# Building a gate table from contiguous float32 one-hots, with 62 instead of 48 expert chunks parked ahead

## The chip, the core and the metric

The kernel runs on one core of one Trainium2 chip. The metric is the device time of one execution, in microseconds. The median of three runs before the change is 1922.45 us (1918.22 to 1923.83).

Engine names as in the profile: PE multiplies matrices (PEld is its loading of the stationary operand), DVE and ACT work element by element, POOL issues the indirect gathers here, SP issues all other DMAs.

## The reference

One encoder layer on 512 tokens of width 1024: a mixer of attention and a gated recurrence, then a retrieval layer over 16384 single-neuron experts, then a gated addition of a per-layer embedding. The change is in the retrieval layer. Cut to what matters:

```python
q = (ht @ w_q).reshape(T, PEER_HEADS, 2, PEER_DKEY // 2)
s = jnp.einsum('thpc,hpnc->thpn', q, sub_keys)
v1, i1 = lax.top_k(s[:, :, 0], K); v2, i2 = lax.top_k(s[:, :, 1], K)     # K = 16 of 128 keys
top_s, pos = lax.top_k(v1[..., :, None] + v2[..., None, :], K)           # 16 pairs a head
idx = i1 * 128 + i2 at pos;  g = softmax(top_s)
a = einsum('thkd,td->thk', u[idx], x)        # 8 heads x 16 experts a token
w = gelu(a) * g
out = einsum('thk,thkd->td', w, v[idx])
```

After it, for every token, x + sigmoid(rmsnorm(x) @ ple_gate) * (p @ ple_proj).

## The kernel before

Tokens are worked in four blocks of 128. Matmuls of full precision are made of three matmuls over operands split into a high and a low part (mm3, lines 133 to 136; split, lines 138 to 141: ACT rounds to the high part, DVE subtracts for the low one).

The retrieval layer treats the blocks in two ways. **Block 0** gathers: for each of its 128 (head, rank) slots one indirect DMA brings 128 rows of u (slot_u), DVE multiplies them with the token's normed vector and sums; later a second one brings the rows of v (slot_v, line 898) and DVE accumulates them into acc. **Blocks 1 to 3** (384 tokens) are dense: the 16384 experts are taken as 128 chunks of 128. For each chunk, dense_a (line 776) computes all products with u in PSUM (pa, 24 matmuls with 384 columns) and takes their gelu (ge). w_prep (line 985) multiplies ge by the chunk's gate table (the softmax weight where a token selected the expert, else zero), splits the product and the chunk of v, and w_mm (line 1010) multiplies them into the six accumulators po (18 matmuls with 512 columns a chunk).

The gate table is built by build (line 850) for one block at a time and written to HBM (gdram), because it is needed chunk by chunk but is made token by token. For each token it is an outer product: a one-hot of the first index (gL) and a one-hot of the second index scaled by the softmax weight (gR), contracted over the 128 slots by one float32 matmul into PSUM (pg; two instructions each). For 8 tokens at a time, DVE compares an iota with the indices into gL (float32, token-major) and gO (bf16, the token innermost), ACT scales gO into gR one token at a time, PE multiplies, ACT moves four tokens' results from pg into the block buffer gs, where the token is innermost, and every 32 tokens gs goes out by DMA. gs has one buffer.

While the tables are built, PE also works through chunks of the first product. Their ge can't be used yet, so the first SP = 48 of them are *parked*: written to HBM (adram, line 958) and read back in w_prep (ges, line 1000). The other 80 are *fresh*, made in the main loop shortly before their use; at most PRE of them wait in SBUF. chunk_order spreads the parked ones over the main loop. Program order follows units of estimated cost: topk and build yield cost units, and one more chunk is emitted for every APACE units (line 967); GPACE, GSTART, GS2 and GP2 pace the u gathers in the same way. The order on each engine is then laid out by the framework's planner, with raised priority for the splits of u (HPU) and the gelu (HPG).

The main loop (line 1018) runs over the 128 chunks: w_prep, fresh chunks as due, w_mm, then u and v gathers of block 0 as due. The table is read back 8 chunks at a time into one buffer (GC, B_GC; line 992). At iteration IT1 = 118 all remaining gathers are emitted, the pools of the first product are closed, and the per-layer embedding's part begins, with block 0's norm and its first gate. The last four chunks' matmuls (LASTN) are done at the end, block by block, so that each block's norm runs beside the next one's matmuls; then the remaining gates run.

Of the kernel before, what the change touches and what calls it, by code (L numbers as in the profile page):

```python
# [28 lines left out]
C_ID, C_IOTA, C_COS, C_SIN, C_RST = 0, 128, 256, 384, 512  # L29
# [3 lines left out]
UEND = 8  # L33
WG = 8
LASTN = 4
GC = 8
B_GC = 1
# [11 lines left out]
PRE = 8  # L49
SP = 48  # L50
TQ = 8
APACE = 3.3
# [7 lines left out]
IT1 = 118  # L60
WLAG = 4
# [24 lines left out]
def const_arrays():  # L86
    c = np.zeros((128, C_END), np.float32)
# [6 lines left out]
    for off, fn in ((C_COS, np.cos), (C_SIN, np.sin)):  # L94
        c[:, off:off + 128] = fn(ang).astype(np.float32).reshape(NT, 128, 32).transpose(1, 0, 2).reshape(128, 128)
    rst = np.ones((8, 128), np.float32)
    rst[:, 0] = 0.0
    c[:, C_RST:C_END] = rst.reshape(-1)[None]
# [27 lines left out]
def body(nc, tc, I, out, taps=None, stop=99):  # L126
# [17 lines left out]
    with contextlib.ExitStack() as top:  # L144
        glob = top.enter_context(tc.tile_pool(name="glob", bufs=1))
        cst = glob.tile([128, C_END], F32, name="cst")
# [49 lines left out]
        if True:  # L196
# [4 lines left out]
            hT_l = fp.tile([128, ND, T], F32R, name="hT_l")  # L201
            ysp = [[fp.tile([128, 4, T], F32R, name=f"{nm}{p}") for p in "hl"] for nm in "oy"]
# [11 lines left out]
            with tc.tile_pool(name="n1", side="right", bufs=1) as n1:  # L214
# [4 lines left out]
                DM.dma_start(cst[:, 0:C_COS], I["cst"][:, 0:C_COS])  # L219
# [7 lines left out]
                DM.dma_start(cst[:, C_COS:C_END], I["cst"][:, C_COS:C_END])  # L227
# [105 lines left out]
            def hgrn_head(h):  # L333
# [5 lines left out]
                V.tensor_tensor_scan(SC.rearrange(fl), cst[:, C_RST:C_END], LF.rearrange(fl), 0.0, OP.mult, OP.add)  # L339
# [144 lines left out]
            for tb in range(NT):  # L484
                for (src, dst, H, o, gg) in ((aq[:, tb, :], qr, 8, 0, qn_g), (akv[:, tb, 0:128], kr, 2, 8, kn_g)):
# [7 lines left out]
                    co, si = [cst[:, off + 32 * tb:off + 32 * tb + 32].rearrange("p (a i) -> p a i", a=2)[:, None]  # L493
# [159 lines left out]
        v8s = [pp.tile([128, 16, 16], F32, name=f"v8_{tb}") for tb in range(NT)]  # L653
        i8s = [pp.tile([128, 16, 16], U32, name=f"i8_{tb}") for tb in range(NT)]
        with s5:
# [49 lines left out]
            ul_st = contextlib.ExitStack()  # L705
            up = [ul_st.enter_context(tc.tile_pool(name="ustr0", side="left", **LR))]
# [50 lines left out]
def peer(nc, tc, I, out, xd, cst, gains, norm_T1, rstd_of, split, mm3, tap, stop, pp, ha, la, h2n, v8s, i8s, st, top,  # L757
# [8 lines left out]
    if True:  # L766
# [83 lines left out]
        def build(kp, bp, ps, tb, i_f, g_o, iob):  # L850
# [3 lines left out]
            tij = kp.tile([128, 2, 128], BF16, name="tij", tag="tij")  # L854
# [3 lines left out]
            for b in range(128 // GB):  # L858
                gs = bp.tile([128, 128, GB], F32, name="gs", tag="gs", bufs=1)
                for q8 in range(GB // TQ):  # L860
                    t0 = b * GB + q8 * TQ
                    LL = bp.tile([128, TQ, 128], F32, name="gL", tag="gL")
                    OO = bp.tile([128, 128, TQ], BF16, name="gO", tag="gO")
                    RR = bp.tile([128, TQ, 128], F32, name="gR", tag="gR")
                    V.tensor_tensor(LL, iob[:, :, 0][:, None, :].to_broadcast([128, TQ, 128]),
                                    tij[:, 0, t0:t0 + TQ, None].to_broadcast([128, TQ, 128]), op=OP.is_equal)
                    V.tensor_tensor(OO, iob, tij[:, 1, None, t0:t0 + TQ].to_broadcast([128, 128, TQ]), op=OP.is_equal)  # L867
                    for t in range(TQ):
                        S.activation(RR[:, t, :], OO[:, :, t], AF.Copy, scale=gr[:, t0 + t:t0 + t + 1])  # L869
                    for q4 in range(TQ // 4):  # L870
                        pg = ps.tile([128, 4, 128], F32, name="pg", tag="pg")
                        for w in range(4):
                            t = q4 * 4 + w
                            PE.matmul(pg[:, w, :], RR[:, t, :], LL[:, t, :], start=True, stop=True)  # L874
                        o = q8 * TQ + 4 * q4
                        S.activation(gs[:, :, o:o + 4].rearrange("p i t -> p t i"), pg, AF.Copy)  # L876
                    yield TQ * 0.21 + 0.1
# [4 lines left out]

        def gather(src, k, tag):
            t = gt.tile([128, D], F32, name=tag, tag=tag)
# [35 lines left out]
        with s7:  # L920
# [3 lines left out]
            iob = kp.tile([128, 128, TQ], BF16, name="iob")  # L924
            V.tensor_copy(iob, iota[:, :, None].to_broadcast([128, 128, TQ]))
# [17 lines left out]
            def units():  # L943
                yield from sel(0)
                yield from sel(1)
                for tb in (1, 2, 3):
                    gens = [build(kp, bp, ps, tb, *sels[tb], iob)]
                    if tb < 3:
                        gens.append(sel(tb + 1))
                    yield from zipped(*gens)  # L950
# [28 lines left out]

        vp = ys.enter_context(tc.tile_pool(name="vstr", side="right", bufs=2, reuse_waits="tile"))  # L980
# [3 lines left out]
        N0 = na  # L984
        def w_prep(it):
            c = it
# [11 lines left out]
            if spilled:  # L998
                ge = vp.tile([128, TD], F32, name="ges", tag="ges", bufs=B_GE)
                DM.dma_start(ge, ad[spidx[c]])  # L1000
# [17 lines left out]
        for it in range(128):  # L1018
# [9 lines left out]
            if it < IT1:  # L1028
                if it >= G0:
                    gathers(GW + (it + 1 - G0) * (128 + WLAG - GW) / (IT1 - UEND - G0), VLEAD + (it + 1 - G0) * 128 / (IT1 - G0), ops[0], ops[5])  # L1030
            if it == IT1:
                gathers(999, 999, ops[0], ops[5])
# [29 lines left out]
                V.tensor_tensor(X[0], X[0], acc, op=OP.add)  # L1062
# [27 lines left out]
                norm_T1(pe2[0], ps1, "p1", X[0], 2, h3h, h3l, "n3", 0, B_XN)  # L1090
                gate(0, 0, *wg0, ps1, "p1")
        for tb in range(3):
# [5 lines left out]
            norm_T1(pe2[0], ps1, "p1", X[tb + TB0], 2, h3h, h3l, "n3", tb + TB0, B_XN)  # L1098
        ys.close()
        with contextlib.ExitStack() as e2:  # L1100
            pe2.append(e2.enter_context(tc.tile_pool(name="ple3", side="right", **LR)))
            ps = e2.enter_context(tc.psum_pool(name="psp", side="right", bufs=4, reuse_waits="tile"))
            for n in range(4):
                w = wg0 if n == 0 else load_wg(n)
                for tb in range(1 if n == 0 else 0, NT):
# [59 lines left out]
```

## Time and profile before

| | us |
|---|---|
| median of three runs | 1922.45 |
| the profiled execution | 1921.56 |
| its span | 1919.8 |
| PE busy in the span | 1841.0 |
| PEld busy | 1619.2 |
| DVE busy | 1416.3 |
| ACT busy | 982.5 |
| POOL busy | 374.3 |

The profile is of one execution. A matmul's busy time runs from its start to its modelled end and matmuls overlap, so a busy PE is not a PE at its peak; the distance from one matmul's start to the next's tells more. The granted TensorE clock was 0.994 over the span. The DMA share is the mean busy share of the core's 16 DMA engines. An idle time is put down to what ended it. In each of the profile's rows, L and a number is a line of the kernel.

### The profile page before, as it was taken

To read this page: it belongs to the slowest core of one execution; us is meant where nothing else is said; L and a number is where in the kernel's file an instruction comes from. 1 tells how busy PE (TensorE), PEld (TensorE's weight loads), DVE (VectorE), ACT (ScalarE), POOL (GpSimd) and SP (SyncE) were. 2 spreads that over 40 slices of the span, in tenths; PEclk is the share of its full clock that TensorE was granted. 3 is DMA by queue.
4 is the path that set the end of the run, shared out by engine and by line. 5 is a ranking of instruction groups with operands and counts; after the bars stand their busy time and mean duration, and the time that the engine had idled before them with its cause. 6 is when DMAs were issued, how large, how long until landed. Compare 5 with 4: busy or idle time off the path is not lost.

```text
span 1919.8 us, 27163 instructions
## 1 busy us (share of the span) xinstructions
PE 1841.0 (96%) x9989; PEld 1619.2 (84%) x9989; DVE 1416.3 (74%) x2893; ACT 982.5 (51%) x1561; POOL 374.3 (19%) x260
## 2 busy tenths in 40 slices
PE   6999999999999999888889999999999999999998
PEld 5997888888887988787778888888888888888888
DVE  3689787444898999988746778887777777656464
ACT  5755656432433589999994334333333333333443
POOL 0000000000000322214301334443354443201000
PEclk9999999999999999999999999999999999999999
DMA  4212100433321776777748998988999988765512
GB/s 161 78 55 78 45 12 23 132 108 129 119 84 60 268 252 239 270 262 266 260 168 307 335 338 318 326 327 319 327 332 341 319 306 324 265 220 177 191 58 86
DMA packets 133941, 397.44 MB, mean 207 GB/s; under 512 B 12848, under 2 KB 52016, under 8 KB 132144
## 3 DMA queue, kind: packets, MB, share of 16 engines
q1 hardware_dynamic: 96944, 261.48, 38.7%
q0 software_dynamic: 36864, 134.23, 19.6%
q8 instruction: 78, 1.28, 0.3%
q14 instruction: 55, 0.45, 0.1%
HBM read 356.86 MB, written 38.80 MB: 206 GB/s over the span
## 4 chain that ended last, share of the span: by engine, by line
PE 45%; ACT 9%; DMA 2%; DVE 1%; issue 0%; ACTq 0%; SPq 0%
PE po L136 9%; PE po L135 9%; PE po L134 9%; PE pa L136 5%; PE pa L135 5%; PE pa L134 5%; ACT gR L869 4%; ACT gs L876 3%; DMA gdram<-gs 1%; ACT u_h L139 1%; PE pg L134 1%; PE pg L136 1%; PE pg L135 1%; DMA gchg<-gdram 1%; ACT ge L784 0%
## 5 line engine op out<-in xcount | busy, mean ns | idle before, releaser
L885 POOL DMA_INDIRECT gu<-in_peer_u_dram,idxg x128 | 191.7, 1498 | 1131.8 <-DVE cd L808 659.5
L136 PE MATMUL pa<-ha,u_l 128*128 128x384 f32 x1024 | 349.4, 341 | 5.5 <-DVE u_l L140 5.5
L134 PE MATMUL pa<-ha,u_h 128*128 128x384 f32 x1024 | 349.3, 341 | 2.2 <-ACT u_h L139 1.8
L135 PE MATMUL pa<-la,u_h 128*128 128x384 f32 x1024 | 348.7, 341 | 0.0
L134 PE MATMUL po<-v_h,w_h 128*128 128x512 f32 x768 | 299.5, 390 | 1.9 <-ACT w_h L139 1.9
L135 PE MATMUL po<-v_l,w_h 128*128 128x512 f32 x768 | 300.8, 392 | 0.0
L136 PE MATMUL po<-v_h,w_l 128*128 128x512 f32 x768 | 300.7, 392 | 0.0
L139 ACT ACTIVATE u_h<-u_raw 128x1024 fp32r<-128x1024 f32 x128 | 136.4, 1066 | 205.8 <-PE pa L135 198.2
L885 POOL DMA_INDIRECT gv<-in_peer_v_dram,idxg x128 | 182.4, 1425 | 239.9 <-DVE acc L900 208.2
L140 DVE TENSOR_TENSOR u_l<-u_raw,u_h 128x1024 fp32r<-128x1024 f32 x128 | 156.2, 1221 | 90.7 <-ACT u_h L139 90.6
L136 PEld LDWEIGHTS pa<-ha,u_l 128*128 128x128 f32 x1024 | 193.3, 189 | 7.6 <-DVE u_l L140 7.4
L134 PEld LDWEIGHTS pa<-ha,u_h 128*128 128x128 f32 x1024 | 193.5, 189 | 6.0 <-ACT u_h L139 2.5
L135 PEld LDWEIGHTS pa<-la,u_h 128*128 128x128 f32 x1024 | 193.3, 189 | 2.8
L874 PE MATMUL pg<-gL,gR 128*128 128x128 f32 x768 | 145.7, 305 | 34.8 <-ACT gs L876 18.3
L140 DVE TENSOR_TENSOR v_l<-v_raw,v_h 128x1024 fp32r<-128x1024 f32 x128 | 155.9, 1219 | 25.5 <-ACT v_h L139 25.5
L869 ACT ACTIVATE gR<-gO,gr 128x128 f32<-128x128 bf16 x384 | 170.0, 547 | 4.1 <-DVE gO L867 4.0
L134 PEld LDWEIGHTS po<-v_h,w_h 128*128 128x128 f32 x768 | 144.5, 188 | 30.8 <-ACT w_h L139 2.2
L136 PEld LDWEIGHTS po<-v_h,w_l 128*128 128x128 f32 x768 | 144.6, 188 | 30.3
L874 PEld LDWEIGHTS pg<-gL,gR 128*128 128x128 f32 x768 | 108.4, 191 | 71.9 <-ACT gR L869 33.5
L135 PEld LDWEIGHTS po<-v_l,w_h 128*128 128x128 f32 x768 | 144.5, 188 | 28.7
L900 DVE SCALAR_TENSOR_TENSOR acc<-gv,aa,acc 128x1024 f32<-128x1024 f32 x128 | 163.7, 1279 | 5.3 <-DMA gv<-in_peer_v_dram,idxg 4.9
L891 DVE SCALAR_TENSOR_TENSOR gu<-gu,h2n 128x1024 f32<-128x1024 f32 x128 | 155.5, 1217 | 6.5 <-DMA gu<-in_peer_u_dram,idxg 6.5
(323 smaller groups left out, 3448.7 us busy)
## 6 DMA issues: line engine op xcount, KB each, us to landing
u_raw<-in_u_t_dram SPq DMA_DIRECT2D x128, 512.0 KB, 5.4
v_raw<-in_peer_v_dram SPq DMA_DIRECT2D x128, 512.0 KB, 6.7
gdram<-gs SPq DMA_DIRECT2D x12, 2048.0 KB, 7.8
gchg<-gdram SPq DMA_DIRECT2D x16, 1536.0 KB, 12.6
w_raw<-in_w_in_dram SPq DMA_DIRECT2D x42, 512.0 KB, 3.6
adram<-ge SPq DMA_DIRECT2D x48, 192.0 KB, 3.3
ges<-adram SPq DMA_DIRECT2D x48, 192.0 KB, 6.5
wq_raw<-in_peer_wq_dram SPq DMA_DIRECT2D x16, 512.0 KB, 3.5
```

What stands on the lines that cost most here:

```text
L134: PE.matmul(ps, lh, rh, start=first, stop=False)
L135: PE.matmul(ps, lh, rl, start=False, stop=False)
L136: PE.matmul(ps, ll, rh, start=False, stop=last)
L139: ins = S.activation(hi, raw, AF.Copy)
L140: V.tensor_tensor(lo, raw, hi.bitcast(F32), op=OP.subtract)
L869: S.activation(RR[:, t, :], OO[:, :, t], AF.Copy, scale=gr[:, t0 + t:t0 + t + 1])
L874: PE.matmul(pg[:, w, :], RR[:, t, :], LL[:, t, :], start=True, stop=True)
L876: S.activation(gs[:, :, o:o + 4].rearrange("p i t -> p t i"), pg, AF.Copy)
L885: G.indirect_dma_start(out=t, out_offset=None, in_=src, in_offset=bass.IndirectOffsetOnAxis(ap=idxg[:, k:k + 1], axis=0))
L891: V.scalar_tensor_tensor(t, t, 1.0, h2n, op0=OP.mult, op1=OP.mult, accum_out=aa[:, k:k + 1])
L900: V.scalar_tensor_tensor(acc, t, aa[:, k:k + 1], acc, op0=OP.mult, op1=OP.add)
```

## The change

The constants table is split: the identity and the iota stay for the whole kernel, the rotary tables and the scan's resets go to a tile cfr that lives only as long as the first part. The top-8 lists move into a pool that is released with the first product's buffers. In build, gL and gO become one float32 tile gE, made by one compare from the float32 iota, the token outside and the key innermost for both indices; gR reads it contiguously; the pg tile has the token innermost, so each matmul writes every fourth float of a bank, and the eviction writes runs of four floats. The bf16 copy of the iota is gone.

62 chunks are parked instead of 48, at one per 2.6 cost units instead of 3.3, and PRE is 7. Parked chunks are asked for three iterations ahead of use. The table is read back four chunks at a time into two buffers. The v gathers get a pool of their own that outlives the first product's; they are spread up to iteration 127, those of u up to IT1; block 0's add, norm and first gate come after block 1's last matmuls and norm, and the gate that runs between is block 1's.

```diff
-GC = 8
-B_GC = 1
+GC = 4
+B_GC = 2
...
-PRE = 8
-SP = 48
+PRE = 7
+SP = 62
 TQ = 8
-APACE = 3.3
+APACE = 2.6
...
+VEND = 128
+GLEAD = 3
...
-        cst = glob.tile([128, C_END], F32, name="cst")
+        cst = glob.tile([128, C_FR], F32, name="cst")
...
+            cfr = fp.tile([128, C_END], F32, name="cfr")
...
-        v8s = [pp.tile([128, 16, 16], F32, name=f"v8_{tb}") for tb in range(NT)]
-        i8s = [pp.tile([128, 16, 16], U32, name=f"i8_{tb}") for tb in range(NT)]
...
+            tp = ul_st.enter_context(tc.tile_pool(name="top8", side="left", **LR))
+            v8s = [tp.tile([128, 16, 16], F32, name=f"v8_{tb}") for tb in range(NT)]
+            i8s = [tp.tile([128, 16, 16], U32, name=f"i8_{tb}") for tb in range(NT)]
...
-            tij = kp.tile([128, 2, 128], BF16, name="tij", tag="tij")
+            tij = kp.tile([128, 2, 128], F32, name="tij", tag="tij")
...
-                    LL = bp.tile([128, TQ, 128], F32, name="gL", tag="gL")
-                    OO = bp.tile([128, 128, TQ], BF16, name="gO", tag="gO")
+                    EE = bp.tile([128, 2, TQ, 128], F32, name="gE", tag="gE")
                     RR = bp.tile([128, TQ, 128], F32, name="gR", tag="gR")
-                    V.tensor_tensor(LL, iob[:, :, 0][:, None, :].to_broadcast([128, TQ, 128]),
-                                    tij[:, 0, t0:t0 + TQ, None].to_broadcast([128, TQ, 128]), op=OP.is_equal)
-                    V.tensor_tensor(OO, iob, tij[:, 1, None, t0:t0 + TQ].to_broadcast([128, 128, TQ]), op=OP.is_equal)
+                    V.tensor_tensor(EE, iota[:, None, None, :].to_broadcast([128, 2, TQ, 128]),
+                                    tij[:, :, t0:t0 + TQ, None].to_broadcast([128, 2, TQ, 128]), op=OP.is_equal)
                     for t in range(TQ):
-                        S.activation(RR[:, t, :], OO[:, :, t], AF.Copy, scale=gr[:, t0 + t:t0 + t + 1])
-                    for q4 in range(TQ // 4):
-                        pg = ps.tile([128, 4, 128], F32, name="pg", tag="pg")
+                        S.activation(RR[:, t, :], EE[:, 1, t, :], AF.Copy, scale=gr[:, t0 + t:t0 + t + 1])
+                    for q in range(TQ // 4):
+                        pg = ps.tile([128, 128, 4], F32, name="pg", tag="pg")
                         for w in range(4):
-                            t = q4 * 4 + w
-                            PE.matmul(pg[:, w, :], RR[:, t, :], LL[:, t, :], start=True, stop=True)
-                        o = q8 * TQ + 4 * q4
-                        S.activation(gs[:, :, o:o + 4].rearrange("p i t -> p t i"), pg, AF.Copy)
+                            t = 4 * q + w
+                            PE.matmul(pg[:, :, w], RR[:, t, :], EE[:, 0, t, :], start=True, stop=True)
+                        o = q8 * TQ + 4 * q
+                        S.activation(gs[:, :, o:o + 4], pg, AF.Copy)
...
-            iob = kp.tile([128, 128, TQ], BF16, name="iob")
-            V.tensor_copy(iob, iota[:, :, None].to_broadcast([128, 128, TQ]))
...
+        gpool["gv"] = ys.enter_context(tc.tile_pool(name="gathv", side="right", bufs=B_G, reuse_waits="tile"))
...
         def w_prep(it):
+            nonlocal nb
+            while nb < min(128, it + 1 + GLEAD):
+                if nb in spidx:
+                    back[nb] = vp.tile([128, TD], F32, name="ges", tag="ges", bufs=B_GE)
+                    DM.dma_start(back[nb], ad[spidx[nb]])
+                nb += 1
...
-                ge = vp.tile([128, TD], F32, name="ges", tag="ges", bufs=B_GE)
-                DM.dma_start(ge, ad[spidx[c]])
+                ge = back.pop(c)
...
-            if it < IT1:
-                if it >= G0:
-                    gathers(GW + (it + 1 - G0) * (128 + WLAG - GW) / (IT1 - UEND - G0), VLEAD + (it + 1 - G0) * 128 / (IT1 - G0), ops[0], ops[5])
+            if it >= G0:
+                gathers(999 if it >= IT1 else GW + (it + 1 - G0) * (128 + WLAG - GW) / (IT1 - G0), (it + 1 - G0) * 128 / (VEND - G0), ops[0], ops[5])
             if it == IT1:
-                gathers(999, 999, ops[0], ops[5])
                 ul_st.close()
...
-                V.tensor_tensor(X[0], X[0], acc, op=OP.add)
...
-                norm_T1(pe2[0], ps1, "p1", X[0], 2, h3h, h3l, "n3", 0, B_XN)
-                gate(0, 0, *wg0, ps1, "p1")
...
             norm_T1(pe2[0], ps1, "p1", X[tb + TB0], 2, h3h, h3l, "n3", tb + TB0, B_XN)
+            if tb == 0:
+                gathers(999, 999)
+                V.tensor_tensor(X[0], X[0], acc, op=OP.add)
+                norm_T1(pe2[0], ps1, "p1", X[0], 2, h3h, h3l, "n3", 0, B_XN)
+                gate(TB0, 0, *wg0, ps1, "p1")
...
-                for tb in range(1 if n == 0 else 0, NT):
+                for tb in (0, 2, 3) if n == 0 else range(NT):
                     gate(tb, n, *w, ps, "pg2")
```

More of the change, by code (lines that the diff above doesn't have):

```diff
@@ L27 @@
 NCELL = sum(ROW_N)
-C_ID, C_IOTA, C_COS, C_SIN, C_RST = 0, 128, 256, 384, 512
+C_ID, C_IOTA, C_FR = 0, 128, 256
+C_COS, C_SIN, C_RST = 0, 128, 256
 C_END = C_RST + 2 * T
@@ L86, in const_arrays @@
 def const_arrays():
-    c = np.zeros((128, C_END), np.float32)
+    c = np.zeros((128, C_FR + C_END), np.float32)
     c[:, C_ID:C_ID + 128] = np.eye(128, dtype=np.float32)
@@ L94, in const_arrays @@
     for off, fn in ((C_COS, np.cos), (C_SIN, np.sin)):
-        c[:, off:off + 128] = fn(ang).astype(np.float32).reshape(NT, 128, 32).transpose(1, 0, 2).reshape(128, 128)
+        c[:, C_FR + off:C_FR + off + 128] = fn(ang).astype(np.float32).reshape(NT, 128, 32).transpose(1, 0, 2).reshape(128, 128)
     rst = np.ones((8, 128), np.float32)
     rst[:, 0] = 0.0
-    c[:, C_RST:C_END] = rst.reshape(-1)[None]
+    c[:, C_FR + C_RST:] = rst.reshape(-1)[None]
     s = np.arange(128)
@@ L218, in body @@
                 DM.dma_start(x1[0], I["x"][0:128, :])
-                DM.dma_start(cst[:, 0:C_COS], I["cst"][:, 0:C_COS])
+                DM.dma_start(cst, I["cst"][:, 0:C_FR])
                 DM.dma_start(gains, I["gains"])
@@ L226, in body @@
                 pre[1280] = wtile(w_in[10], (8, 128))
-                DM.dma_start(cst[:, C_COS:C_END], I["cst"][:, C_COS:C_END])
+                DM.dma_start(cfr, I["cst"][:, C_FR:C_FR + C_END])
                 r = rstd_of(n1, ss, NT, 1.0 / D, "n1")
@@ L338, in hgrn_head @@
                 fl = "p a t -> p (a t)"
-                V.tensor_tensor_scan(SC.rearrange(fl), cst[:, C_RST:C_END], LF.rearrange(fl), 0.0, OP.mult, OP.add)
+                V.tensor_tensor_scan(SC.rearrange(fl), cfr[:, C_RST:C_END], LF.rearrange(fl), 0.0, OP.mult, OP.add)
                 S4 = SC.rearrange("p a (c j) -> p a c j", c=4)
@@ L492, in body @@
                     x1, x2 = s5[:, :, :, 0, :], s5[:, :, :, 1, :]
-                    co, si = [cst[:, off + 32 * tb:off + 32 * tb + 32].rearrange("p (a i) -> p a i", a=2)[:, None]
+                    co, si = [cfr[:, off + 32 * tb:off + 32 * tb + 32].rearrange("p (a i) -> p a i", a=2)[:, None]
                               .to_broadcast([128, H, 2, 16]) for off in (C_COS, C_SIN)]
@@ L848, in topk, with build @@
             yield 0.6
-        def build(kp, bp, ps, tb, i_f, g_o, iob):
+        def build(kp, bp, ps, tb, i_f, g_o):
             pt = ps.tile([128, 3, 128], F32, name="pt3", tag="pt3", bufs=1)
@@ L881, in peer @@
         un, vn = I["peer_u"], I["peer_v"]
+        gpool = {"gu": gt}
         def gather(src, k, tag):
-            t = gt.tile([128, D], F32, name=tag, tag=tag)
+            t = gpool[tag].tile([128, D], F32, name=tag, tag=tag)
             G.indirect_dma_start(out=t, out_offset=None, in_=src,
@@ L946, in units @@
                 for tb in (1, 2, 3):
-                    gens = [build(kp, bp, ps, tb, *sels[tb], iob)]
+                    gens = [build(kp, bp, ps, tb, *sels[tb])]
                     if tb < 3:
@@ L984, in peer @@
         N0 = na
+        back = {}
+        nb = 0
         def w_prep(it):
+            nonlocal nb
[4 more added lines that the diff above has]
+                nb += 1
             c = it
```

## The prediction

> **What bounds the kernel now.** I read the busy times by stretch first, because the page's whole-span shares mix stages with different limits. Columns: stretch, its length, then busy us (and instruction count) of PE, PEld, DVE, ACT and POOL, the granted clock, the DMA share, GB/s.
>
> ```profile
> 620.00:685.00 65.00, 62.44 (x348) 60.29 (x348) 63.22 (x247) 33.43 (x40) 17.21 (x14) 0.99 0.72 261
> 685.00:1003.00 318.00, 283.16 (x1645) 246.03 (x1644) 264.60 (x454) 303.13 (x564) 80.69 (x52) 0.99 0.68 242
> 1003.00:1026.00 23.00, 21.55 (x123) 20.90 (x121) 9.39 (x11) 9.38 (x13) 0.00 (x0) 1.00 0.85 299
> 1026.00:1050.00 24.00, 23.18 (x95) 19.02 (x96) 19.45 (x31) 12.61 (x18) 3.70 (x3) 0.93 0.88 303
> 1050.00:1100.00 50.00, 50.00 (x233) 42.70 (x232) 36.57 (x48) 16.52 (x27) 18.84 (x13) 1.00 0.98 359
> 1100.00:1700.00 600.00, 600.00 (x2970) 537.94 (x2969) 464.00 (x576) 215.22 (x303) 248.83 (x170) 1.00 0.89 318
> 1700.00:1750.00 50.00, 50.00 (x249) 44.82 (x248) 29.23 (x34) 17.63 (x25) 4.81 (x4) 1.00 0.53 176
> 1750.00:1820.00 70.00, 70.00 (x332) 60.68 (x331) 35.49 (x41) 26.85 (x37) 0.00 (x0) 1.00 0.52 183
> 1820.00:1920.00 100.00, 93.25 (x600) 83.79 (x598) 52.68 (x132) 39.54 (x80) 0.00 (x0) 0.99 0.22 74
> ```
>
> From 1050 to 1820 PE never rests and nothing but less PE work can shorten it. From 685 to 1003, the stage that builds the gate table (I call it B), ACT is busy 303 of 318 us. PE's 283 there is deceptive, so I counted its real work: the same stretches for tile pa alone (PE, PEld, ACT), then for pg alone.
>
> ```profile
> 620.00:685.00 65.00, 62.28 (x345) 59.97 (x345) 6.67 (x14) 0.99 0.72 261
> 685.00:1003.00 318.00, 190.51 (x871) 149.79 (x870) 18.16 (x36) 0.99 0.68 242
> ```
>
> ```profile
> 685.00:1003.00 318.00, 145.74 (x768) 108.42 (x768) 103.43 (x96) 0.99 0.68 242
> ```
>
> Next, the timeline where PE alone sets the pace (three u_h splits, each released by the chunk before), the timeline inside B, and a piece of the chain of waits in B.
>
> ```profile
> 1007.15 1.06 ACT L139 ACTIVATE u_h<-u_raw 128x1024 fp32r<-128x1024 f32 x1 [2.64 <-PE pa L135]
> 1011.31 1.06 ACT L139 ACTIVATE u_h<-u_raw 128x1024 fp32r<-128x1024 f32 x1 [2.72 <-PE pa L135]
> 1015.47 1.06 ACT L139 ACTIVATE u_h<-u_raw 128x1024 fp32r<-128x1024 f32 x1 [2.72 <-PE pa L135]
> ```
>
> ```profile
> 870.40 3.42 ACT L869 ACTIVATE gR<-gO,gr 128x128 f32<-128x128 bf16 x8 [1.01 <-DVE gO L867]
> 872.64 1.12 PEld L874 LDWEIGHTS pg<-gL,gR 128*128 128x128 f32 x6
> ```
>
> ```profile
> 968.36 0.95 ACT u_h L139
> 969.30 0.38 ACT ge L784
> 969.68 0.96 ACT gs L876
> 970.69 1.17 PE pg L874 x8
> ```
>
> An expert chunk of the first product (24 pa matmuls) takes PE 4.16 us (1011.31 - 1007.15), 0.173 us a matmul. Where nothing holds PE up, eight pg instructions take 1.17 us; taking off the last one's own 0.30 us (its mean is below) leaves 0.87 for seven, 0.124 each. Inside B six pg weight loads take 1.12, 0.19 each, because two of them wait for every gR, and ACT makes a gR each 3.42 / 8 = 0.43 us. So B holds 871 x 0.173 = 151 us of pa and 768 x 0.124 = 95 us of pg: 246 us of PE work in 318. **72 us of PE are lost in B behind ACT**, most of it hidden inside "busy". 620 to 685 holds 345 x 0.173 = 59.8 us of work in 65, so 8% is lost there, where DVE (63 of 65) runs beside PE.
>
> **The change, part by part.** The prices: groups by shape (busy us, mean ns | idle before).
>
> ```profile
> L869 ACT ACTIVATE gR<-gO,gr 128x128 f32<-128x128 bf16 x384 | 170.0, 547 | 4.1 <-DVE gO L867 4.0
> L876 ACT ACTIVATE gs<-pg 128x512 f32<-128x512 f32 x96 | 103.7, 1126 | 3.3 <-DMA gdram<-gs 2.2 <-PE pg L874 1.0
> L865 DVE TENSOR_TENSOR gL<-iob,tij 128x1024 f32<-128x1024 bf16 x48 | 96.4, 2007 | 16.1 <-PE pg L874 14.9 <-ACT tij L855 1.1
> L867 DVE TENSOR_TENSOR gO<-iob,tij 128x1024 bf16<-128x1024 bf16 x48 | 32.8, 683 | 13.0 <-ACT gR L869 12.9
> L874 PE MATMUL pg<-gL,gR 128*128 128x128 f32 x768 | 145.7, 305 | 34.8 <-ACT gs L876 18.3 <-ACT gR L869 15.1 <-DVE gL L865 0.8
> L140 DVE TENSOR_TENSOR u_l<-u_raw,u_h 128x1024 fp32r<-128x1024 f32 x128 | 156.2, 1221 | 90.7 <-ACT u_h L139 90.6
> L555 ACT ACTIVATE PTt<-ptp 128x512 f32<-128x512 f32 x32 | 18.8, 598 | 13.4 <-PE ptp L553 13.3
> L900 DVE SCALAR_TENSOR_TENSOR acc<-gv,aa,acc 128x1024 f32<-128x1024 f32 x128 | 163.7, 1279 | 5.3 <-DMA gv<-in_peer_v_dram,idxg 4.9
> ```
>
> From the answers for three single lines, min/median/max in ns:
>
> ```profile
> L820 ACT ACTIVATE g_o<-g_o x3: 311/311/312, 657.8 to 824.3; 128x128 f32<-128x128 f32 x3
> L351 DVE TENSOR_TENSOR DD<-tot,SC x4: 1204/1210/1224, 51.9 to 267.5; 128x1024 f32<-128x1024 f32 x4
> L487 DVE TENSOR_TENSOR aq<-aq,rr_a x4: 677/682/691, 160.9 to 181.1; 128x512 f32<-128x512 f32 x4
> ```
>
> *gR.* It reads 128 contiguous float32 instead of every eighth bf16. The nearest row, L820 (128 float32, SBUF to SBUF), lasts 0.311; gR lasts 0.547 and follows itself at 0.43, an overlap of 0.12, so the new pace is about 0.19. The saving lies between nothing and 384 x 0.24 = 92 us; L820 is almost the new shape, so I take 75.
>
> *gs.* It writes runs of four floats instead of single floats 128 bytes apart. Between nothing and 96 x (1.126 - 0.598) = 51 us (L555 is the contiguous eviction of that size); I take 30, nearer to L555 since a run replaces each lone element.
>
> *One-hots.* One 128x2048 float32 compare replaces gL (2.007) and gO (0.683). From L487 and L351, which both broadcast one operand, 512 more elements cost 0.528 us, so 2048 cost 1.210 + 2 x 0.528 = 2.27. Dearest: two of gL's, 4.01, if broadcasting was what made gL slow; the float32 broadcasts of L351 and L487 speak against that. DVE gains 48 x (2.69 - 2.27) = 20 us; at the dear end it loses 64. The two-deep one-hot buffer is now held until both the gR copies and the matmuls have read it; both come sooner.
>
> *62 parked chunks, every 2.6 instead of 3.3 cost units.* 14 chunks, 14 x 4.16 = 58 us of PE, leave the stage where PE is never idle. The pace is even, and of the 161 units that the yields add up to (19 in each of four selections, 28.5 in each of three builds) 38 come before the first build, so about 3 land ahead of B and 11 in B. Each costs ACT 0.95 + 0.38 and DVE 1.22. In B:
> - ACT: 303 - 75 - 30 + 11 x 1.33 = 213 us.
> - DVE: 265 - 20 + 11 x 1.22 = 258 us.
> - PE: 246 + 11 x 4.16 = 292 us, now the most loaded.
>
> With 8% lost, as from 620 to 685, B takes 315 us: 3 less than before, with 11 chunks more. The stretch ahead of it, 17.4 chunks x 4.16 x 1.08 = 78, takes 13 more. 14 chunks gone from the rest: -58. **Sum: -3 + 13 - 58 = -48 us.**
>
> *Parked chunks asked for 3 ahead; table 4 chunks at a time, two buffers.* Answers of the DMA list (KB each, us to landing) and of the waits:
>
> ```profile
> gchg<-gdram SPq DMA_DIRECT2D x16, 1536.0 KB, 12.6
> ...
> ges<-adram SPq DMA_DIRECT2D x48, 192.0 KB, 6.5
> ```
>
> ```profile
> DVE ges L1003 <- DMA gchg<-gdram: 59.2, 13, 6.9
> ...
> DVE ges L1003 <- DMA ges<-adram: 20.2, 9, 6.4
> ```
>
> These DVE waits (79 us) end none of PE's: PE is 600 of 600 busy while they happen, w_h and w_l being four deep. Worth 0 now; they remove what would be late next, since an iteration of the main loop gets shorter. On SP's queue a ges issue moves ahead of later v_raw and table issues, and the earlier request meets a ring of four; SP issues 44 DMAs more (16 for the table, 14 parked writes, 14 parked reads). DMA: the rows from 1026 to 1820 move 238 MB in 794 us (length by GB/s, summed). 14 chunks of u (7 MB) leave the stage, 14 parked reads (3 MB) come to it, and 234 MB must pass in 736 us, 318 GB/s. If pieces of half the length cost as much each, the 25 MB table (16 x 1536 KB) counts double: 352. The stretch 1050 to 1100 shows 359 with PE busy throughout. Worth 0, at worst some stalls.
>
> *Gathers to the end, block 0 last.* The gathered block's v reads now end with iteration 127 instead of 117; block 0's add, norm and first gate move behind block 1's, and block 1's gate takes the place of block 0's. 16 gates and four norms before and after. From 1750 to 1820 POOL is at 0 and DVE at 35 of 70 us, so some 18 accumulations of 1.28 us fit (58 of 70). Late acc would hold block 0's transposes, and behind them on PE the last matmuls of blocks 2 and 3. I take 0, at worst 10 us.
>
> *Memory moves.* The rotary and reset constants, and the top-8 lists, change pools with the same bytes and instructions; the bf16 copy of iota (one instruction before B) goes. 0.
>
> The profiled execution took 1921.6 us (span 1919.8), 0.9 under the median of 1922.45. 1921.6 - 48 = 1873.6; forecast **1873 us**.
>
> **The rivals.**
> 1. *A strided PSUM write slows the pg matmuls.* They now write every fourth float of a bank. No row shows PE doing that. Below: nothing, since a pg instruction at 0.124 for 128 columns takes 0.97 ns a column, against pa's 0.173 / 384 = 0.45, so a write twice as slow could still hide. Above: the ratio of gs to L555, 1.88, on all of it: 768 x 0.109 = 84 us on PE, in the stage PE now sets. At half the loss (4%, PE alone being late), B = (292 + 84) x 1.04 = 391: +73 + 13 - 58 = +28, **1950 us**. It turns into a slowdown once B exceeds 363, that is from 0.20 us per instruction ((363 / 1.04 - 292) / 768 = 0.074 more). I take nothing, by the column rate.
>
> The Trainium skill says the opposite: "PSUM — Partial Sum Buffer", Specifications (TRN2), gives 8-byte lines and says any non-contiguous pattern slows matmuls significantly. No run here shows it yet; by that rule this rival is the result.
>
> 2. *ACT gets no faster.* gR and gs keep their times: ACT in B is 303 + 15 = 318, at its present 95% busy 334 us. +16 + 13 - 58 = -29, **1893**. Against it: L820 and L555.
> 3. *The compare costs two gL's.* DVE in B is 265 + 64 + 13 = 342, at 95% 360: +42 + 13 - 58 = -3, **1919**. Against it: L351, L487.
> 4. *The end or the DMA gives some back*: 10 us for a late acc and 10 for stalls, **1893**. For it: DMA at 0.89 to 0.98 from 1050 on. Against: PE without a gap there.
>
> **How the numbers follow.** Forecast 0.63, rival 1 0.14, rival 2 0.09, rival 3 0.07, rival 4 0.07. The forecast's own range: with no loss in either stretch, B 292 and 72 ahead, -26 + 7 - 58 = -77 (1845); with 12% lost, B 327, 81 ahead, +9 + 16 - 58 = -33 (1889). The 0.8 range takes in rivals 2 and 4 and stops short of 3 and 1: 1846 to 1912. A measurement here can't tell less than 0.3% (6 us) from no change. Faster: 0.63 + 0.09 + 0.07 + 0.01 of rival 1's mild end = 0.80; same 0.07 (rival 3); slower 0.13.
>
> **What would show it.** Right: gR near 0.3 us and gs near 0.6 to 0.8; the compare near 2.27; eight free pg still 1.2 us; the last pg near 1015 with 62 chunks parked; PE as full as before from there to the end, and that stretch 58 us shorter. Wrong: pg weight loads 0.2 us apart without a wait for gR (rival 1); pg still waiting for gR (2); pg waiting for gE with DVE full (3); PE idle on v_raw, u_raw or X[0] (4).

## The result, and the profile after

| | before | after |
|---|---|---|
| median of 4 runs each, us | 1922.51 (1918.22 to 1923.83) | 1947.30 (1937.79 to 1952.33) |
| ratio, 95% interval | | 1.0127 [1.0079, 1.0175] |
| profiled execution, us (span) | 1921.56 (1919.8) | 1951.74 (1950.0) |
| mean granted clock | 0.994 | 0.979 |

The changed kernel is 25 us slower where 48 us less were forecast. First the part that went as planned: groups by shape, after (busy us, mean ns | idle before).

```profile
L872 ACT ACTIVATE gR<-gE,gr 128x128 f32<-128x128 f32 x384 | 121.1, 393 | 28.3 <-DVE gE L869 28.3
L869 DVE TENSOR_TENSOR gE<-cst,tij 128x2048 f32<-128x2048 f32 x48 | 109.2, 2284 | 18.6 <-PE pg L877 18.6
L877 PE MATMUL pg<-gE,gR 128*128 128x128 f32 x768 | 107.5, 284 | 9.0 <-ACT gR L872 4.5 <-ACT gs L879 4.4
L879 ACT ACTIVATE gs<-pg 128x512 f32<-128x512 f32 x96 | 54.9, 590 | 19.0 <-DMA gdram<-gs 11.8 <-PE pg L877 5.8 <-issue 1.1
```

gR and gs together cost ACT 98 us less (170.0 + 103.7 before), and PE waits 9 us ahead of pg instead of 35. Now the busy times by stretch, after; columns as before: length, busy us (count) of PE, PEld, DVE, ACT, POOL, granted clock, DMA share, GB/s.

```profile
685.00:988.00 303.00, 291.37 (x1901) 285.46 (x1900) 258.22 (x418) 238.04 (x586) 82.17 (x54) 0.99 0.77 283
988.00:1050.00 62.00, 58.10 (x277) 51.12 (x276) 40.67 (x59) 25.73 (x42) 12.01 (x11) 0.97 0.97 330
1050.00:1100.00 50.00, 43.06 (x194) 36.61 (x193) 33.82 (x44) 15.28 (x20) 15.57 (x13) 0.93 0.85 304
1100.00:1700.00 600.00, 545.43 (x2558) 480.40 (x2558) 401.12 (x506) 184.29 (x261) 224.18 (x151) 0.95 0.81 281
```

The build stage is shorter, 303 us instead of 318, and PE issues 1901 matmuls in it instead of 1645. The loss stands in the main loop: from 1100 to 1700 PE was busy 600.00 of 600 us with 2970 matmuls before, and now 545.43 with 2558, at a mean clock of 0.95. DMA carries less than before (0.81 against 0.89, 281 GB/s against 318), so its engines aren't fuller than they were. The waits that end in that stretch (us in total, times, longest):

```profile
ACT v_h L142 <- DMA v_raw<-in_peer_v_dram: 177.0, 37, 12.9
ACT w_h L142 <- DVE ge L1015: 120.6, 20, 15.3
DVE ges L1015 <- DMA ges<-adram: 85.4, 16, 9.8
DVE ges L1015 <- DMA gchg<-gdram: 79.5, 10, 9.5
...
PE pa L139 <- DVE u_l L143: 46.6, 11, 6.9
...
DVE ges L1015 <- issue: 30.6, 5, 7.6
...
PE po L138 <- DVE v_l L143: 8.0, 7, 2.3
...
DVE u_l L143 <- ACT u_h L142: 3.0, 2, 2.1
```

All of PE's idle time there (54.6 us) ends with u_l or v_l, the low parts of a chunk of u or v, which DVE makes. DVE stands 165 us (85.4 + 79.5) in front of the products of *parked* chunks (ges): for the parked chunk itself, or for its table piece. At five more of these products the profile names no cause ("issue", 30.6 us); the trace's packets show that each time the last packet of a parked chunk had ended 0.6 to 0.7 us before, so these are waits for parked chunks too, 196 us of waits for loads in all. With them DVE has no time left: 401 us busy, 196 for loads, 3 for other engines. One such place in the DVE timeline (start, length, ..., idle before and what ended it), with SP's requests and PE around it:

```profile
1303.83 0.56 DVE L1015 TENSOR_TENSOR ges<-ges,gchg 128x384 f32<-128x384 f32 x1 [8.23 <-DMA gchg<-gdram]
...
1308.66 1.22 DVE L143 TENSOR_TENSOR u_l<-u_raw,u_h 128x1024 fp32r<-128x1024 f32 x1
...
1316.55 0.55 DVE L1015 TENSOR_TENSOR ge<-ge,gchg 128x384 f32<-128x384 f32 x1
...
1321.03 1.21 DVE L143 TENSOR_TENSOR v_l<-v_raw,v_h 128x1024 fp32r<-128x1024 f32 x1
1331.69 0.56 DVE L1015 TENSOR_TENSOR ges<-ges,gchg 128x384 f32<-128x384 f32 x1 [9.45 <-DMA gchg<-gdram]
1332.17 0.55 DVE L143 TENSOR_TENSOR w_l<-ges,w_h 128x384 fp32r<-128x384 f32 x1
```

```profile
1317.12 0.75 SPq L1005 DMA_DIRECT2D gchg<-gdram  x1
1322.27 1.40 SPq L1007 DMA_DIRECT2D v_raw<-in_peer_v_dram  x1
1332.75 0.33 SPq L997 DMA_DIRECT2D ges<-adram  x1
```

```profile
1307.02 0.34 PE L138 MATMUL pa<-la,u_h 128*128 128x384 f32 x1
1309.94 0.45 PE L139 MATMUL pa<-ha,u_l 128*128 128x384 f32 x1 [2.58 <-DVE u_l L143]
...
1311.09 0.33 PE L139 MATMUL pa<-ha,u_l 128*128 128x384 f32 x1
...
1311.53 0.52 PE L138 MATMUL pa<-la,u_h 128*128 128x384 f32 x1
1311.85 0.52 PE L139 MATMUL pa<-ha,u_l 128*128 128x384 f32 x1
```

DVE takes its instructions in order: its 512 low parts and gate products start in the trace in the order of the compiled program. The product at 1316.55 is the last reader of a table buffer; 0.6 us later SP can ask for the next piece (1317.12), and only five instructions further on (the last is the v_l that ends at 1322.24) stands the product that needs it. DVE waits 9.45 us. SP stands too: its next request gets out at 1332.75, right behind the w_l that starts at 1332.17. The wait before, which ends at 1303.83, shows what PE makes of it: u_l, behind it on DVE, ends at 1309.88, PE runs dry for 2.58 us until 1309.94, and a little later its matmuls come 0.32 us apart instead of 0.17, at the granted half clock. With two buffers the request should come a whole piece ahead. Why it doesn't is shown by the order of the products on DVE around this place (from the compiled program; numbers rise in program order, gchg is the piece):

```
ges_12090 <- gchg_12262      ges_12192 <- gchg_12262
ge_11856  <- gchg_12053      ge_11923  <- gchg_12053
ges_12332 <- gchg_12474      ges_12437 <- gchg_12474
ge_12030  <- gchg_12262      ge_12134  <- gchg_12262
```

(Read it line by line, left before right.) The planner has put the parked products of each piece ahead of the fresh ones of the piece *before*. So the first user of a new piece stands right behind the last user of the buffer that it takes. Counted over the program, it is the 5th to 7th DVE instruction behind it at 14 pieces in a row (with the one buffer before: the 4th to 9th at every piece); the second buffer's lead is used up by the order. The four buffers of the parked chunks fare likewise: at 31 of 58 places the next parked product is at most the 5th DVE instruction behind the one that frees its buffer (before: at 8 of 44).

### The profile page after: what moved, and what is told of

Its sections match the earlier page's. It is cut to its first block, busy times and chain, and to the rows that moved or that the text cites. A ratio compares the mean times of both kernels' runs of the same rounds, so it can differ in the third digit from the quotient of the medians.

```text
span 1950.0 us, 27242 instructions
## 1 busy us (share of the span) xinstructions
PE 1831.4 (94%) x9989; PEld 1631.2 (84%) x9989; DVE 1391.7 (71%) x2844; ACT 899.9 (46%) x1561; POOL 385.9 (20%) x260
## 2 busy tenths in 40 slices
DMA packets 162806, 402.96 MB, mean 207 GB/s; under 512 B 13552, under 2 KB 80880, under 8 KB 161008
## 5 line engine op out<-in xcount | busy, mean ns | idle before, releaser
L139 PE MATMUL pa<-ha,u_l 128*128 128x384 f32 x1024 | 356.0, 348 | 55.2 <-DVE u_l L143 55.2
L137 PE MATMUL pa<-ha,u_h 128*128 128x384 f32 x1024 | 355.0, 347 | 0.3 <-ACT u_h L142 0.3
L138 PE MATMUL pa<-la,u_h 128*128 128x384 f32 x1024 | 352.9, 345 | 0.0
L139 PEld LDWEIGHTS pa<-ha,u_l 128*128 128x128 f32 x1024 | 198.7, 194 | 63.1 <-DVE u_l L143 62.7
L890 POOL DMA_INDIRECT gv<-in_peer_v_dram,idxg x128 | 194.1, 1517 | 289.4 <-DVE acc L905 182.2
L142 ACT ACTIVATE v_h<-v_raw 128x1024 fp32r<-128x1024 f32 x128 | 134.7, 1054 | 243.5 <-DMA v_raw<-in_peer_v_dram 220.0
L1015 DVE TENSOR_TENSOR ges<-ges,gchg 128x384 f32<-128x384 f32 x62 | 34.2, 556 | 251.9 <-DMA ges<-adram 129.9
L137 PEld LDWEIGHTS pa<-ha,u_h 128*128 128x128 f32 x1024 | 198.3, 194 | 3.1 <-ACT u_h L142 0.6
L138 PEld LDWEIGHTS pa<-la,u_h 128*128 128x128 f32 x1024 | 198.3, 194 | 2.3
L872 ACT ACTIVATE gR<-gE,gr 128x128 f32<-128x128 f32 x384 | 121.1, 393 | 28.3 <-DVE gE L869 28.3
```

Of the source, the lines that this page charges most:

```text
L137: PE.matmul(ps, lh, rh, start=first, stop=False)
L138: PE.matmul(ps, lh, rl, start=False, stop=False)
L139: PE.matmul(ps, ll, rh, start=False, stop=last)
L142: ins = S.activation(hi, raw, AF.Copy)
L872: S.activation(RR[:, t, :], EE[:, 1, t, :], AF.Copy, scale=gr[:, t0 + t:t0 + t + 1])
L890: G.indirect_dma_start(out=t, out_offset=None, in_=src, in_offset=bass.IndirectOffsetOnAxis(ap=idxg[:, k:k + 1], axis=0))
```

## The experiments

Each time is a median, and each ratio stands against runs of the kernel before on the same chip (medians 1919.9 to 1921.8). "Built on" says what a diff is against. "Waits for loads" are DVE's waits from 1100 to 1700 that a DMA ended, and those ahead of a gate product for which the profile names no cause ("issue"): at all of these the last packet of a parked chunk had ended 0.5 to 1.0 us before. The letters of the theories are explained in the texts on what was expected; P and Q mean one thing at b_onehot62 and another from b_two on.

### One part at a time

**One-hots alone (b_onehot).** The kernel before with the change's build, constants and lists; 48 parked, the table by 8, parked chunks and gathers as they were. The constants, against the changed kernel:

```diff
-GC = 4
-B_GC = 2
-PRE = 7
-SP = 62
-APACE = 2.6
+GC = 8
+B_GC = 1
+PRE = 8
+SP = 48
+APACE = 3.3
```

> The kernel before with the float32 one-hots, their pg layout and the memory moves alone; 48 parked chunks, the main loop as before. If ACT alone held PE up while the table is built: that stage, with 246 us of PE work, shrinks from 318 to 255 to 270 us, and the whole to 1865 to 1880 us. If a strided write slowed the pg matmuls: pg instructions 0.2 us apart, 1900 us or more.

1866.27 us, ratio 0.9712 [0.9695, 0.9728]. Rows of the stretches, columns as above:

```profile
685.00:952.00 267.00, 256.97 (x1691) 247.12 (x1690) 248.77 (x408) 227.21 (x566) 99.74 (x52) 0.99 0.82 293
...
1100.00:1700.00 600.00, 600.00 (x2969) 537.69 (x2968) 451.42 (x556) 214.29 (x302) 240.97 (x159) 1.00 0.86 307
```

The build stage ends near 952 instead of 1003, and the main loop is as full as before. This part alone brings 54 us.

**The table by 4 on the kernel before (b_gc4).**

```diff
-GC = 8
-B_GC = 1
+GC = 4
+B_GC = 2
```

> The kernel before with nothing but the table read 4 chunks at a time into two buffers. Theory 1: stalls like those of the changed kernel appear in the main loop, 1950 to 2010 us. Theories 2 and 3: 1915 to 1930, since nothing is asked for ahead and the loop is no shorter.

1978.64 us, ratio 1.0296 [1.0273, 1.0318]. Two waits of the stretch from 1100 to 1700:

```profile
DVE ges L1003 <- DMA gchg<-gdram: 103.9, 14, 10.1
...
DVE ges L1003 <- DMA ges<-adram: 56.9, 9, 9.9
```

Before, the two were 57.8 (12 waits) and 13.6 (4). The waits for the table are hardly more, 14 instead of 12, but longer, and those for parked chunks are 9 instead of 4 and longer too. These two constants cost 59 us, without any other part of the change.

**The change with the table by 8 (a_gc8).** Built on the changed kernel: the reverse of the diff above.

> The changed kernel with the table read 8 chunks at a time into one buffer again. Theory 1 (small pieces: a piece of 4 chunks has as many packets as one of 8, each half as long, and takes as long to land, 14 us, so DVE, and SP's queue behind the piece, are held twice as often): PE's gaps of 70 us and most of the 84 us of halved clock after 1000 us go, 1860 to 1880 us. Theory 2 (parked chunks asked for 3 ahead delay v_raw on SP's queue): stays at 1940 to 1950. Theory 3 (a shorter main loop with gathers up to its end asks more than the DMA gives): stays at 1930 to 1950.

1893.79 us, ratio 0.9845 [0.9814, 0.9875]: 53 us come back, less than the 1860 to 1880 us that were given for small pieces as the only cause, and the change without its table part is 1.5% faster than the kernel before.

**Parked chunks not asked for ahead (a_lead0).** Built on the changed kernel: `-GLEAD = 3`, `+GLEAD = 0`.

> The changed kernel with each parked chunk asked for in its own iteration. Theory 1: 1935 to 1965 us, no better, perhaps worse. Theory 2: 1860 to 1890. Theory 3: 1930 to 1950.

1941.01 us, ratio 1.0097 [1.0079, 1.0115], within the changed kernel's own spread: it isn't the cause.

**62 parked chunks (b_onehot62), and asked for 3 ahead (b_onehot62lead).** Built on b_onehot:

```diff
-PRE = 8
-SP = 48
-APACE = 3.3
+PRE = 7
+SP = 62
+APACE = 2.6
```

> The kernel before with the one-hots and with 62 parked chunks at 2.6 units, PRE 7; table, requests and gathers as before. Theory P (with the one-hots PE is full in both stages, so a chunk moved from one to the other is worth nothing): 1860 to 1875 us. Theory Q (14 more parked reads in a main loop whose DMA is already at 0.9 give new stalls there): 1880 to 1900, with PE gaps after 1000 us.

> The same, and parked chunks are asked for three iterations ahead; only the gathers' new pace and end are then missing against the changed kernel with the table read by 8. If the request ahead is what costs that kernel its last 27 us: 1885 to 1900. If the gathers are: like the kernel without the request ahead, within 6 us. If the request does its work: 5 us or more faster than without.

1891.81 us (0.9857 [0.9840, 0.9874]) and 1895.80 us (0.9876 [0.9860, 0.9893]). Parking 14 more chunks *costs* 25.5 us, as given there for new stalls, and asking ahead brings nothing. Between 1100 and 1700, b_onehot62:

```profile
1100.00:1700.00 600.00, 576.50 (x2762) 511.69 (x2761) 440.81 (x552) 202.02 (x284) 244.78 (x164) 0.98 0.86 308
```

So the steps from before to after are: one-hots -54, parking +26, asking ahead +4, gathers last and the rest -2, the table by 4 +53.

### Why the table by 4 is dear

**Asked one piece earlier in the program (a_tab, b_onehot_tab).** The request for a piece stands four iterations ahead of its first use; b_onehot_tab is b_onehot with the table by 4 in that manner.

```diff
-            if key not in gch or c % GC == 0:
-                ...
+            if c % GC == 0:
+                for c0 in ([c, c + GC] if c == 0 else [c + GC]):
+                    ...
```

> The changed kernel (table 4 chunks at a time, two buffers), with each piece asked for one whole piece, four iterations, ahead. Theory R (the pieces are asked for too late, and DVE's wait for them holds the rest): waits for the table gone, 1880 to 1905 us, like the changed kernel with pieces of 8. Theory S (twice the packets fill the DMA engines, so that v_raw, u_raw and ges behind them are late however early the piece is asked for): waits for the table gone, but v_raw and ges as late as before, 1925 to 1950.

> The one-hot kernel (48 parked, gathers as before) with the table 4 chunks at a time into two buffers, each piece asked for one piece ahead. Theory R: 1855 to 1872 us, at least as fast as with pieces of 8 (1866). Theory S: 1885 to 1925.

1940.12 us (1.0116 [1.0097, 1.0135]) and 1918.26 us (0.9984 [0.9971, 0.9997]). Asking earlier in the text changes nothing to speak of: in a_tab the distance on DVE is the same 5 to 7 instructions at the same 14 pieces, since the request still needs the buffer. On b_onehot the table by 4 costs 52 us.

**Packets, requests, SP's queue.** Built on b_onehot, each piece of 8 chunks as two requests: halves by chunk (b_two) or by token group (b_halves).

```diff
+                for h in (0, GC // 2):                  # b_two
+                    DM.dma_start(gch[key][:, :, h:h + GC // 2, :], ...)
+                for hb in (slice(0, NTB // 2), slice(NTB // 2, NTB)):   # b_halves
+                    DM.dma_start(gch[key][:, hb], ...)
```

> The kernel before with the one-hots alone (48 parked, table 8 chunks at a time, 1866 us), with each table piece asked for as two requests, 4 chunks each, one right behind the other into the two halves of the same buffer: rows of 512 B, twice the packets and twice the requests, at the old rhythm of every eighth chunk. Theory N (the price goes by the number of packets that the DMA engines have to take): about as dear as the table read 4 chunks at a time there (1918), 1905 to 1930. Theory R (the price goes by the rhythm: a piece that the next multiply waits for, every 4 chunks instead of every 8): as without it, 1862 to 1872. Theory Q (the price goes by the number of requests on SP's queue): 1905 to 1930 too.

> The same kernel (1866 us) with each table piece asked for as two requests of 6 of its 12 token groups: rows of 1024 B as before, the packets unchanged, twice the requests. Theories N and R: 1862 to 1872. Theory Q: 1905 to 1930.

1865.97 us (0.9707 [0.9685, 0.9728]) and 1866.89 us (0.9718 [0.9697, 0.9738]). Twice the packets or twice the requests at the old rhythm cost nothing, so neither their number (N) nor that of the requests (Q) is the price. Larger pieces and another queue:

```diff
-GC = 8
+GC = 16                                   # b_onehot62g16, on b_onehot62
-                DM.dma_start(gch[key], gd...
+                S.dma_start(gch[key], gd...   # a_actq, on the changed kernel
```

> One-hots and 62 parked chunks (1892 us), with the table read 16 chunks at a time into one buffer: rows of 2048 B, half the packets, half the requests. Theory N: 12,288 packets less, half of what 24,576 more cost (53), so about 1866, 1855 to 1875, and PE fuller than 576 of 600 us from 1100 to 1700. If instead a piece of twice the size, 3 MB, holds the multiply for twice as long at each of 8 places: 1892 to 1910.

> The changed kernel (1947 us) with its table pieces issued by ACT instead of SP, so that on no queue a chunk of v or of u stands behind a table piece. If the price is that the next chunks of v and u wait behind the piece in SP's queue: 1900 to 1925, with the waits for v_raw well under their 220 us. Theory N: 1940 to 1960, the waits spread otherwise.

1889.81 us (0.9829 [0.9808, 0.9850]) and 1947.97 us (1.0116 [1.0078, 1.0154]). Half the packets bring nothing. With the table on ACT's queue the waits for v_raw fall from 220 to 55 us over the whole span, as hoped, and the time stays: those waits were a consequence.

**The order on DVE (a_ring, b_onehot_tab_ring, b_onehot62_tab_ring).** The product goes to a tile of its own; a_ring, on the changed kernel, has two instead of four buffers for the parked chunks to make room.

```diff
-            mi = V.tensor_tensor(ge.rearrange(...), ge.rearrange(...), ..., op=OP.mult)
+            gw = vp.tile([128, TD], F32, name="gw", tag="gw", bufs=2)
+            mi = V.tensor_tensor(gw.rearrange(...), ge.rearrange(...), ..., op=OP.mult)
+            ge = gw
```

> The changed kernel (1947 us) with the gate product written into a tile of its own with two buffers, instead of in place (and two buffers instead of four for the parked chunks, for room), so that the planner can't put a parked chunk's product ahead of older chunks: a piece's first product then stands some 26 DVE instructions behind the product that frees its buffer, instead of 6. Theory H (the hoisted parked product waits for a piece that was just asked for, and holds DVE with all that is behind it; with 4 chunks a piece this comes twice as often): the waits for the table on DVE fall from 91 us to under 25, the time to that of the 8-chunk table or less, 1870 to 1900. Theory P (the requests and small pieces as such load the DMA): 1940 or more, the waits moved elsewhere.

> The kernel before with the one-hots and the table read 4 chunks at a time (1918 us), with the gate product in a tile of its own with two buffers. Theory H: back to the 1866 of the 8-chunk table, 1855 to 1875. Theory P: 1910 to 1925.

> One-hots and 62 parked chunks (1892 us), with the table read 4 chunks at a time into two buffers and the gate product in a tile of its own. If 62 parked chunks cost 25 because their products, too, are hoisted into table waits: 1835 to 1870, below the 1866 with 48. If they cost 25 by the load on the DMA alone: 1885 to 1900.

1861.88 us (0.9692 [0.9675, 0.9708]), 1863.45 us (0.9707 [0.9691, 0.9723]) and 1863.31 us (0.9700 [0.9683, 0.9716]). The products now stand in program order on DVE; in a_ring a piece's first user is the 15th to 36th DVE instruction behind the one that frees its buffer, and a parked product never nearer than the 7th behind its own. In none of the three does DVE wait for a DMA from 1100 to 1700, and PE is full. The row of a_ring:

```profile
1100.00:1700.00 600.00, 600.00 (x2933) 533.09 (x2932) 463.83 (x573) 215.76 (x302) 218.18 (x161) 1.00 0.91 314
```

With the same 403 MB and the same 162,806 packets as the changed kernel, a_ring is 85 us faster, so the load on the DMA (theory P) isn't the price. And the 25.5 us of 62 parked chunks are gone too: with the products in order, 48 and 62 give 1863.45 and 1863.31.

**Fewer parked buffers, in place (a_ge2).** Built on the changed kernel: `-B_GE = 4`, `+B_GE = 2`.

> The changed kernel (1947 us) with two buffers instead of four for the parked chunks and nothing else: the planner then hoists by one chunk at most places, and a first product stands 14 to 28 DVE instructions behind the one that frees its buffer at 24 of 30 places. Theory H: 1880 to 1915. Theory P: 1940 or more.

1947.52 us (1.0139 [1.0108, 1.0170]): a miss for theory H (the order of the products on DVE), which gave 1880 to 1915. No wait for the table is left in the stretch, but another has taken its place, the parked chunks asked for late:

```profile
DVE ges L1015 <- DMA ges<-adram: 183.6, 33, 9.1
```

With two buffers and the product in place, 54 of 60 parked products are at most the 5th DVE instruction behind the one that frees their buffer. So what counts is how long DVE stands, whichever load it stands for.

**More parked buffers, in place (b_onehot_tab_ge6), and the short distance in order (a_gc8_ring).** The tile of its own also frees the parked chunks' buffers earlier. Built on b_onehot_tab and on a_ring:

```diff
-B_GE = 4
+B_GE = 6          # b_onehot_tab_ge6
-GC = 4
-B_GC = 2
+GC = 8            # a_gc8_ring
+B_GC = 1
```

> One-hots and the table 4 chunks at a time (1918 us), the product in place as before, with six buffers for the parked chunks instead of four: as much memory as the tile of its own took. Theory H (the order on DVE): the first products still stand 5 to 8 DVE instructions behind the one that frees their buffer, now at every place to the end, so 1912 to 1930. Theory F (the tile of its own helped because the buffers of the parked chunks come free earlier): 1860 to 1880.

> The changed kernel with the product in a tile of its own (1862 us), the table 8 chunks at a time into one buffer again. With one buffer a piece can't be asked for before the last product of the piece before it, so its first product stands 5 to 7 DVE instructions behind, whatever the order. Theory H: table waits on DVE of some 60 us stay, and it is slower than with 4 chunks and two buffers, 1872 to 1895. Theory F: 1855 to 1868.

1914.27 us (0.9965 [0.9945, 0.9986]) and **1856.34 us (0.9664 [0.9648, 0.9681])**, the fastest of all. A row of the waits from 1100 to 1700 of each, in that order:

```profile
DVE ges L1005 <- DMA gchg<-gdram: 163.9, 23, 9.9
```

```profile
DVE gw L1016 <- DMA gchg<-gdram: 50.2, 11, 8.5
```

More parked buffers in the hoisted order (parked products moved ahead) bring 4 us at most, as H said and against theory F, by which the tile of its own helped because the parked buffers come free earlier. a_gc8_ring is a miss for H, and its time is the one that F gave (1855 to 1868): the table waits stay, as H expected, but they cost nothing, and the waits for parked chunks, 68.5 us in a_gc8, are gone. What the two and all the others have in common is seen when the waits are put beside PE (before and b_gc4 lack the one-hots and so are some 54 us longer elsewhere):

| kernel | DVE's waits for loads, of 600 us | DVE's waits for other engines | PE busy, of 600 us | us |
|---|---|---|---|---|
| a_ring, b_onehot_tab_ring, b_onehot62_tab_ring | 0 | 124 to 148 | 600.0 | 1861.9, 1863.5, 1863.3 |
| a_gc8_ring | 54 | 81 | 600.0 | 1856.3 |
| b_two, b_onehot, before, b_halves | 73, 75, 75, 80 | 64 to 70 | 600.0 | 1866.0, 1866.3, 1922.5, 1866.9 |
| a_gc8, b_onehot62, b_onehot62lead, b_onehot62g16 | 139 to 145 | 10 to 30 | 574.1 to 579.0 | 1889.8 to 1895.8 |
| b_onehot_tab_ge6, b_onehot_tab, b_gc4 | 181, 184, 185 | 0 | 570.5, 562.7, 557.2 | 1914.3, 1918.3, 1978.6 |
| after, a_lead0, a_tab, a_ge2, a_actq | 196 to 207 | 0 to 3 | 538.3 to 549.7 | 1940.1 to 1948.0 |

Where PE is full, DVE is busy 448 to 473 us of the 600 (464.00 before, 463.83 in a_ring). So DVE has some 130 to 150 us to wait, and where loads take little of it, it waits for other engines instead. Up to 80 us of waiting for loads cost PE nothing in any kernel; from 139 on (none lies between) PE runs dry, and from 181 on DVE has nothing else left to give: waiting in order, it sets the pace.

## Why the prediction was wrong

**The build stage: right.** It was forecast at 315 us and took about 303 with PE at 291.37 (forecast 292), DVE at 258.22 (258) and ACT at 238.04 (213). gR saved 49 us where 75 were taken, gs 49 where 30 were; the compare lasts 2.284 us (2.27). Together the two terms of ACT give 98 of 105.

The 13 us that the stretch ahead of this stage was to take more didn't come: the first pg instruction stands at 686.4, before at 687.8.

**The strided PSUM write: free.** Rival 1's time, 1950 us, is near the measured one, but its mechanism isn't there. In a row of the timeline of after, 13 weight loads take 1.59 us, (1.59 - 0.19) / 12 = 0.117 each, under the 0.124 of before and far from the 0.20 at which the rival decides:

```profile
866.53 1.59 PEld L877 LDWEIGHTS pg<-gE,gR 128*128 128x128 f32 x13
```

The Trainium skill's rule ("PSUM — Partial Sum Buffer", Specifications (TRN2): any non-contiguous pattern slows matmuls significantly) isn't borne out for these float32 matmuls of 128 columns.

**The sum of -48: near in size, partly by luck.** One-hots alone give -54, and the whole change with its products in order -58.6 (1920.5 to 1861.9). But the terms were other ones. Forecast were -3 for the build stage, +13 ahead of it and -58 behind it; from before to a_ring the profiled executions show about -15 (303 against 318), -1 and -44 (1861.1 - 988 against 1919.8 - 1003), so misses of 12 to 14 us in both directions. Nor were the 14 chunks that leave the main loop a gain of their own: with 48 parked the gain is the same. Where PE is full on both sides, a chunk moved from one to the other gains nothing; the gain is the PE time that was lost behind ACT in the build stage.

**The table and the parked reads: the step that failed.** It said "These DVE waits (79 us) end none of PE's: PE is 600 of 600 busy while they happen", "Worth 0 now", and, of the smaller pieces, "Worth 0, at worst some stalls". Measured: +53 for the table, +26 for the parking, and PE busy 545.43 of 600 where it was to stay full. Three things were wrong in it.
- It priced the transfers by bytes and GB/s. The runs show that twice the packets, twice the requests and another queue change nothing here (b_two, b_halves, a_actq).
- It took a second buffer and an earlier request to shorten a wait. The planner moved the parked products up to the request. From 1100 to 1700 the waits for the table went from 12 of 4.8 us on average to 10 of 8.0, and those for parked chunks from 4 to 21 (13.6 to 116 us).
- It looked for cover on PE and in w_h, "four deep", and not on the engine that waits. The rows it quoted nearly had the number: DVE 464 busy in 600, and its waits for loads were 75 there, so there was room for some 60 us more. The change added 120. The rest came out of DVE's work, 401 us instead of 464, or 0.86 of it, and PE's matmuls fell alike, 2558 from 2970.

**Rival 4** named the right place, PE idle in the main loop, but put it down to the DMA's load and gave it 10 us. **The end** was right as far as is shown: gathers last, block 0 last and the rest together come to -2 us.

## What to carry to other kernels

Add an in-order engine's waits for loads to its busy time, stretch by stretch: a wait that costs nothing today is spent slack, and when the sum comes to the length of the stretch, each further wait is paid in full. A second buffer gives a lead only as far as the order of its readers leaves one; read the instruction order of the engine before you count on it, above all where some operands come from memory and others from a slower engine, so that a planner may move the former ahead. A result written to a tile of its own instead of in place kept the order here, freed the parked buffers earlier, and was worth 85 us.

## What the runs showed of the hardware

PE's granted clock went to one half around quite short gaps, for 3.4, 6.8 or 10.2 us. In the changed kernel the gap of 2.58 us at 1307.4 was followed by 3.41 us at 0.5, beginning 1.4 us after PE had resumed; gaps of 6.3 to 6.9 us brought 6.8 or 10.2 us; of the gaps from 2.0 to 2.6 us some had none (2.50 at 1583.4). By an estimate from the count of matmuls, half clock took 22 us of the stretch from 1100 to 1700 beside the 55 that PE was idle: 2558 matmuls at a_ring's 600 / 2933 us are 523 us of work, done in 545 busy. Before, with PE full, no record of half clock lies in that stretch. The Trainium skill ("TensorE: Matmul & The Clock Gate", Part 1) has the clock fall after an idle window of about 3.4 us; here 2.3 us were enough at times.

A table piece of half the size didn't land sooner while DVE stalled on it. From the packets of the trace, a piece asked for between 1100 and 1650 had landed after a median of 12.7 us before (8 chunks) and 12.6 in b_onehot_tab_ge6 (4 chunks), where a median of 256 and 322 gather packets of 4 KB, in that order, began between the piece's first packet and its last; in b_onehot_tab_ring, with 55 of them, it took 6.3. That the gathers are what holds the piece up isn't shown by a run of its own.

Left open: a_gc8_ring is 5.5 us faster than a_ring, and no run says why. That the planner moves parked products up because their operands are ready early in its plan is argued from the order; the tile of its own does two things, it keeps the products in order and frees the parked buffers earlier. That the order is what counts for the table by 4 rests on b_onehot_tab_ge6, which gave more buffers and gained 4 us at most; a_gc8_ring, where the table waits stay and those for parked chunks go, speaks for the buffers too. No run has the order without the earlier release, so their shares stay open; both act through DVE's waits.
